# One more convolution pair through the seven-product form of a Trainium2 decoder trunk, with the recurrent heads, the token blocks and one held copy moved to fit

## The chip, the cores and the metric

The kernel runs on one core of a Trainium2 chip. The metric is the device time of one execution in microseconds (us). Two kinds of time appear below: the time of whole runs, and the span of one profiled execution, which is the trace that all rows come from. In the trace PE is TensorE's matmul row and PEld its weight loads, DVE is VectorE, ACT is ScalarE, POOL is GpSimd, and SP is SyncE, whose queue here does nothing but issue DMAs. A line such as L725 is a line of the kernel before.

## The reference

One decoder layer in float32 over 1024 tokens of width 1024:

```python
h = rms_norm(x, g_mix)
va, ga, xb, gb, sa, sb = split(h @ w_in + b_in)        # 1024, 1024, 1536, 1536, 1024, 1024 columns
u = silu(layer_norm(causal_conv31(va * sigmoid(ga))))   # width 31, depthwise
y_a = u @ w_a_out
v = rg_lru(causal_conv4(xb))                            # 16 heads of 96: two gates, then a linear scan
y_b = (v * gelu(gb)) @ w_b_out
x = x + (sigmoid(sa) * y_a + sigmoid(sb) * y_b) @ w_o
h = rms_norm(x, g_mlp)
x = x + square(relu(h @ w_1)) @ w_2
out = rms_norm(x, g_final)
```

The gates of `rg_lru` are two block-diagonal products with a sigmoid; the scan's decay is an exponential of one gate, and its input is scaled by a square root.

## The kernel before, in words

**Precision.** Every float32 operand is split into a high part and a low part (`float32r`), and a product is made of three matmuls: high by high, high by low, low by high. A matmul has a moving operand of 128x512. The high part is a copy on ACT. The low part is made in one of two ways: by a subtraction on DVE, or by `split_dma` (L63), which writes the negated source with ACT, adds the source to it with an accumulating DMA that POOL issues (L66), and then makes the high copy with a second ACT pass. The first way costs one ACT pass and one DVE pass, the second two ACT passes and a DMA.

**The in-projection, first part.** `w_in` has 56 column tiles of 128. The list `CH` (L686) orders those that are done one at a time; a turn `s` of the loop at L810 does one of them with 24 products for each half of the tokens, 48 matmuls (`chunk_mm`, L716). Three tiles are done before the loop, so the turns are 3 to 25. Column names are offsets (L427): VA and GA are the two sides of the gated convolution branch, XB the recurrent branch, GB, SA and SB the three gates. A turn also carries what follows from earlier tiles:

- an XB tile is copied out by two ACT passes in the next turn (`xb_out`, L468), convolved over 4 taps by DVE, and split by `xb_parts` (L489) in the turn after that;
- a GA tile gets its sigmoid on ACT in the next turn, and DVE multiplies it with the VA tile (`u_gate`, `u_mul`, `u_out`, L585 to L598), which makes one of eight convolution inputs `u`. The two last tiles stand in reverse order, GA ahead of VA (L689), so that the sigmoid is done while the last tile is multiplied;
- a recurrent head has two gate products. `HS0` (L796) names the turn in which each head's first product is issued, at the end of that turn; its second follows in the middle of the next turn, and both use one PSUM buffer, so each waits for ACT's sigmoid of the one before (`head_mm`, `head_gate`, L526 and L537);
- four heads make a group. In the turn after a group's last head (`EXP`, L799) ACT does the exponentials and tanh (`scan_exp`), a turn later the square roots (`scan_root`), and DVE does three `scan_tile`s (L573) in the turns after that;
- DVE's free time is filled with the taps of the width-31 convolutions (`conv`, L602), some 47 instructions each.

**Token blocks.** The second part multiplies 2x2 blocks of tokens by 2x2 blocks of weights with Strassen's seven products. It needs differences of token blocks: `x_load` (L662) fetches four blocks for each of two halves `c2` from a DRAM copy through SP's queue, `x_sum` (L668) does four DVE subtractions, and `x_parts` (L673) splits blocks 7, 6, 5 and 4. `XS` (L800) places these steps in the last five turns, and `ZX` (L1021) places the three last ones beside the first products of the second part.

**The in-projection, second part.** `ZPAIRS` (L729) lists pairs of column tiles, 15 of them, of which the seventh is the convolution pair VA+7 with GA+7. A pair takes 7 products of 12 matmuls (`z_mm`, L921). `zseq` (L779) writes out the order of the products, the first two pairs interleaved: products 1, 1, 2, 2, 6, 7, 7, 5, 6, 3, 4, 5. Weight sums are DVE work (`z_sums`), the splits of the left operands are `z_lhs` (L763), issued four products ahead, and `z_post` (L992) copies and evacuates.

**What sets the order.** Every engine executes its instructions in the order of the program text (a manual schedule). A small planner keeps a clock for PE, ACT and DVE, and uses it only to choose how many convolution taps go between the DVE steps that must be done (`later`, `vector_work`, L695 and L699). The pool `acts` (L36) has 37 buffers of 128x1024; when a tile is asked for, its first writer waits for the last user of the buffer it gets. The PSUM pool of the first part has three two-bank buffers under the tag `ps` and one under `ps2`, which the heads use (L47); its tags lie one after another in the order of their first use, and the second part's eight banks lie over them.

**The down-projection.** From L2143 the MLP's second product is done in seven products as well, for two halves `q2` of the tokens. The result of the first product, in `d0a`, is copied to `d0b` (`down_add`, L2016), and the second product then goes on adding into `d0a`. The copy of half 1 is kept in `held` and issued a step later. In steps m = 2, 3 and 4 of group 0 (`joint`) a held step that meets an even step is issued late, after the operand splits of that step and after the first half's matmuls.

Of the kernel before, what the change touches and what calls it, by code (L numbers as in the profile page):

```python
# [12 lines left out]
AF = mybir.ActivationFunctionType  # L13
ALU = mybir.AluOpType
# [5 lines left out]
NH = 16  # L20
# [10 lines left out]
def trunk_kernel(ctx: ExitStack, tc: tile.TileContext, x, xt_in, xt_eo, vecs, w_in, w_a_out, w_b_pl, w_b_sq,  # L31
                 w_rg, w_o, w_1, w_2, g_final, out):

    nc = tc.nc
# [9 lines left out]
    def T(name, dt=F32, shape=(P, S)):  # L44
        return tp.tile(list(shape), dt, tag="T", name=name)

    def PS(name, tag="ps"):  # L47
        return pp.tile([P, S], F32, tag=tag, name=name, bufs=1 if tag == "ps2" else 3)
# [286 lines left out]
    with tc.manual_schedule(engines={mybir.EngineType.Activation, mybir.EngineType.DVE,  # L335
                                     mybir.EngineType.PE}):
        warm = cp.tile([P, 10], F32, name="warm")
        nc.vector.memset(warm[:, 0:2], 1.0)
        nc.scalar.activation(warm[:, 0:1], warm[:, 1:2], AF.Sqrt)

        spare = PS("spare", "ps2")

        def idle_mm(n):
            for _ in range(n):
                nc.tensor.matmul(spare[:, 0:P], ones, ones, start=True, stop=True)

        idle_mm(13)
        rb["tile"] = PS("rb", "ps2")
        first_w(0, "h")
        first_w(0, "l")  # L350
        for c in range(8):
            x_plain(c)
            x_plain_low(c)
            if c == 7:
                first_w(1, "h")
                first_w(1, "l")
            for which in ("hh", "lh", "hl"):
                first_z(0, 0, c, which)
        for k in range(8):
            first_z(1, 0, k, "hh")  # L360
            first_z(1, 0, k, "hl")
        decay_on(6)
        first_w(2, "h")
        first_w(2, "l")
        decay_on(14)
        for t in range(4, 8):
            x_square(t, nc.scalar)
        for k in range(8):
            first_z(1, 0, k, "lh")
        x_root(1)  # L370
        decay_on(5)
        for k in range(8):
            first_z(2, 0, k, "hh")
            first_z(2, 0, k, "hl")
            if k == 4:
                x_spread(1)
        for k in range(8):
            first_z(2, 0, k, "lh")

        for c in range(9):  # L380
            if c < 8:
                x_scaled(1, c)
            else:
                x_root(0)
                x_spread(0)
            if 3 <= c < 7:
                x_square(c - 3, nc.scalar)
            if c:
                for which in ("hh", "lh"):
                    first_z(0, 1, c - 1, which)  # L390
                x_low(1, c - 1)
                first_z(0, 1, c - 1, "hl")
                for i in range(1, N0):
                    first_z(i, 1, c - 1, "hh")
                    first_z(i, 1, c - 1, "hl")
        for i in range(1, N0):
            for k in range(8):
                first_z(i, 1, k, "lh")
        decay()
        nc.vector.tensor_scalar(cab2, cab_c, 2.0, None, ALU.mult)  # L400
        pairs = caw[:, 8:].rearrange("p (i o j) -> p i o j", o=2, j=8)
        nc.vector.tensor_tensor(csum, pairs[:, :, 0, :], pairs[:, :, 1, :], ALU.add)
# [32 lines left out]
    def at(e, cost, ready=0.0):  # L435
        clk[e] = max(clk[e], ready) + cost
        return clk[e] + 0.1
# [144 lines left out]
    yd = dp.tile([8, P, S], F32, name="yd")  # L582
    ysum = []

    def u_gate(j, ps):  # L585
        ut[j] = u = T(f"u{j}")
        nc.scalar.activation(u.rearrange("p (o n) -> p o n", o=2), ps.rearrange("p (n o) -> p o n", o=2),
                             AF.Sigmoid, bias=bin_c[:, GA + j:GA + j + 1])
        return at("A", 1.11)

    def u_mul(j, ps, ready=0):
        uv = ut[j].rearrange("p (o n) -> p o n", o=2)
        later(ready, 1.28, nc.vector.scalar_tensor_tensor, uv, ps.rearrange("p (n o) -> p o n", o=2),
              bin_c[:, VA + j:VA + j + 1], uv, ALU.add, ALU.mult)
        fresh.append(j)

    def u_out(j, psv, psg):
        u_mul(j, psv, u_gate(j, psg))  # L598

    NE = WA // 2 + 1  # L600

# [71 lines left out]
    def x_parts(c2, *ps):  # L673
        for p in ps:
            src = xq[c2][{6: 22, 7: 12, 5: 11, 4: 21}[p]]
            xbh[p][c2] = h = T(f"xs{p}h_{c2}", F32R)
            xbl[p][c2] = l = T(f"xs{p}l_{c2}", F32R)
            if c2 == 0 and p < 6:
                split_dma(src, h, l)
                at("A", 2.0)  # L680
            else:
                nc.scalar.activation(h, src, AF.Copy)
                later(at("A", 1.0), 1.2, nc.vector.tensor_tensor, l, src, h.bitcast(F32),
                      ALU.subtract)

    CH = [XB, VA, GA, XB + 1, XB + 2, VA + 1, GA + 1, XB + 3, XB + 4, XB + 5, VA + 2, GA + 2]  # L686
    CH += [XB + t for t in range(6, 12)] + [c for j in range(3, 7) for c in (VA + j, GA + j)]
    NU = 7
    CH[-2:] = CH[:-3:-1]  # L689
    NC1 = len(CH)  # L690
    zps = {n: z0[n] for n in range(N0)}
    wraw, wst = {}, {}
# [2 lines left out]
    def later(ready, cost, f, *a):  # L695

        todo.append((ready, len(todo), cost, f, a))
# [28 lines left out]
                                 start=n == 0, stop=n == 23)  # L726
        at("P", len(halves) * (n1 - n0) * MM)

    ZPAIRS = [GB + 2 * i for i in range(6)] + [VA + 7] + [SA + 2 * i for i in range(4)]  # L729
    ZPAIRS += [SB + 2 * i for i in range(4)]  # L730
    NZ = len(ZPAIRS)
    zraw, zs, zo, zb = {}, {}, {}, {}
# [58 lines left out]
    def z_get(n, f):  # L791
# [1 line left out]

    ENGINES = {mybir.EngineType.Activation, mybir.EngineType.DVE, mybir.EngineType.PE,
               mybir.EngineType.SP, mybir.EngineType.Pool}
    HS0 = [4 + n + (n > 3) + (n > 7) for n in range(NH)]  # L796
    head_at = {s: n for n, s in enumerate(HS0)}

    EXP = {head_slot: g for g, head_slot in enumerate(HS0[4 * g + 3] + 1 for g in range(4))}  # L799
    XS = {NC1 - 5: ((x_load, 0),), NC1 - 4: ((x_sum, 0),), NC1 - 3: ((x_load, 1), (x_parts, 0, 6)),  # L800
          NC1 - 2: ((x_sum, 1), (x_parts, 0, 7, 5)), NC1 - 1: ((x_parts, 0, 4), (x_parts, 1, 6))}
    made = []
    head_w(0)
    w_load(3)
# [4 lines left out]
    with tc.manual_schedule(engines=ENGINES):  # L809
        for s in range(3, NC1):  # L810
# [31 lines left out]
            if c >= XB:  # L842
                xb_out(c - XB, zps[s - 1])
            elif c >= GA:
                if CH[s] == c - GA + VA:
                    u_gate(c - GA, zps[s - 1])
                else:
                    u_out(c - GA, zps[s - 2], zps[s - 1])
            w_parts(s + 1)
            if before is not None:  # L850
                head_gate(before, 1, clk["P"] - (2 * (24 - mid) + 6) * MM)
# [166 lines left out]
        elif p == 4:  # L1018
            z_out(i, 1, 0, zb[i, "u"], "c")

    ZX = {0: ((x_parts, 1, 7),), 2: ((x_parts, 1, 5),), 4: ((x_parts, 1, 4),)}  # L1021
    H_AT = {2: (0, 0), 5: (1, 1), 3: (0, 1), 4: (1, 0)}
    with tc.manual_schedule(engines=ENGINES):

# [152 lines left out]
        vector_work(clk["V"])  # L1177
        z_get(2, z_lhs)
        z_get(3, z_lhs)
        u_mul(NU - 1, zps[NC1 - 1])  # L1180
        vector_work(clk["V"])
        z_h(0, 0, 0)
        for n in range(len(zseq) + 2):
# [949 lines left out]
    with tc.manual_schedule(engines={mybir.EngineType.Activation, mybir.EngineType.DVE,  # L2133
                                     mybir.EngineType.PE}):
        for n, (g, p, kk) in enumerate(dseq[:-2]):
            m = n % 14
            end = g == NC_ - 1
            nx, nx2 = dseq[n + 1], dseq[n + 2]
            if m in DLOADS and not end:
                d_load(g + 1, *DLOADS[m])  # L2140
            elif m == 0:
                d_load(g, *DFIRST)
            if n == 0:  # L2143
                for q2 in range(2):
                    acc[0, 0, q2] = x_block(0, 0, q2)
            if (g, m) in XADD:
                xbs[g, m] = x_block(*XADD[g, m])
            joint = not g and m in (2, 3, 4)
            if held and not (joint and kk == 0):
                held.pop()()  # L2150
            lows_ = []
            if not end or m < 10:
                lows_.append(left_high(*nx))
            sums_ = d_sums(g, m)
            if sums_ and not joint:
                d_sum(*sums_.pop(0))
            if not end or m < 10:
                lows_.append(right(*nx2))
            down_mm(g, p, kk, 0)
            if joint:  # L2160
                for f in lows_:
                    f()
                if held:
                    held.pop()()
                for x in sums_[::-1]:
                    d_sum(*x)
            if kk:
                if end and p == 7:
                    d_last(0)
                else:  # L2170
                    down_add(g, p, 0)
            if not joint:
                for f in lows_:
                    f()
                for x in sums_:
                    d_sum(*x)
            if (g, m - 4) in XADD:
                k = XADD[g, m - 4]
                tt(acc[k], acc[k], xbs.pop((g, m - 4)), ALU.add)
            down_mm(g, p, kk, 1)  # L2180
# [101 lines left out]
```

## Time and profile before

| | |
|---|---|
| median of 3 runs | 1532.88 us (1532.06 to 1533.77) |
| the profiled execution | 1532.83 us, its span 1531.0 us |
| matmuls | 6722, PE busy 1519.7 us |
| first part's loop | from 43 to 339.1 us of the span |
| second part | 339.1 to 625.8 us |
| granted TensorE clock | 0.998 |

Times inside the trace are counted from the start of the span. Rows of the timeline give start, duration, engine, line, operation, tiles (with buffer numbers left out), and in brackets how long the engine was idle before and what ended that. Successive matmuls of 512 columns start 0.227 us apart, although each has a latency of 0.39 us.

### The profile page before, as it was taken

The page shows a single profiled execution, that of the slowest core. Times are in us where ns is not written, and L with a number is a line of the kernel's source. Part 1 is how long each engine was busy: PE and PEld are TensorE (multiplying, and loading weights), DVE is VectorE, ACT ScalarE, POOL GpSimd, SP SyncE. Part 2 cuts the span into 40 slices and gives each one's busy share as a digit, 9 for nine tenths or more (in the row PEclk, how much of TensorE's full clock was granted, in tenths as well). Part 3 has the DMA queues.
Part 4 walks back from the last instruction along what each step waited for, and adds up shares of the span by engine and source line. Part 5 has one row for each costly group of instructions (what it writes and reads, how often), then busy time and mean ns, then how long its engine had stood idle before and what let it go on. Part 6 is the DMA issues. An engine that isn't in the chain of part 4 may idle for free.

```text
span 1531.0 us, 18964 instructions
## 1 busy us (share of the span) xinstructions
PE 1519.7 (99%) x6722; PEld 1250.9 (82%) x6722; DVE 1200.4 (78%) x1636; ACT 928.2 (61%) x1299; POOL 192.3 (13%) x228
## 2 busy tenths in 40 slices
PE   9999999999999999999999999999999999999998
PEld 7878887888888888888888887888888878888886
DVE  6999996998999997788768879755555386777777
ACT  6748688576566667645475777554444445545475
POOL 0111011022222222000022332000000000101010
PEclk9999999999999999999999999999999999999999
DMA  9766778697997789863779897333333974776465
GB/s 351 189 145 158 180 171 190 200 257 211 265 257 175 183 207 280 295 224 124 265 194 301 191 209 193 129 129 112 112 113 111 305 254 126 182 206 169 108 123 153
DMA packets 130799, 296.53 MB, mean 194 GB/s; under 512 B 12896, under 2 KB 34912, under 8 KB 130704
## 3 DMA queue, kind: packets, MB, share of 16 engines
q1 hardware_dynamic: 98960, 215.92, 41.5%
q0 software_dynamic: 31600, 79.15, 28.1%
q8 instruction: 52, 0.85, 0.2%
q14 instruction: 43, 0.35, 0.1%
q10 hardware_dynamic: 144, 0.26, 0.0%
HBM read 149.79 MB, written 60.82 MB: 138 GB/s over the span
## 4 chain that ended last, share of the span: by engine, by line
PE 95%; issue 2%; DMA 1%; DVE 1%; ACT 1%; POOL 1%; SPq 0%; POOLq 0%; DVEq 0%; ACTq 0%
PE z L725 16%; PE z L258 2%; PE d2b L2002 2%; PE d1b L2002 2%; PE d0b L2002 2%; PE d3b L2002 2%; PE d0e L2002 1%; PE d3a L2002 1%; PE d2e L2002 1%; PE d2a L2002 1%; PE d1e L2002 1%; PE d1a L2002 1%; PE d3e L2002 1%; PE rg L532 1%; PE rg L534 1%
## 5 line engine op out<-in xcount | busy, mean ns | idle before, releaser
L725 PE MATMUL z<-xh,win_h 128*128 128x512 f32 x368 | 115.4, 391 | 0.0
L725 PE MATMUL z<-xl,win_h 128*128 128x512 f32 x368 | 114.9, 390 | 0.0
L637 DVE SCALAR_TENSOR_TENSOR y<-u,vec,y 128x511 f32<-128x511 f32 (+14 forms) x120 | 88.6, 738 | 0.0
L725 PE MATMUL z<-xh,win_l 128*128 128x512 f32 x368 | 87.4, 389 | 0.0
L637 DVE SCALAR_TENSOR_TENSOR yt<-u,vec,yt 128x511 f32<-128x511 f32 (+6 forms) x112 | 82.8, 739 | 0.0
L637 DVE SCALAR_TENSOR_TENSOR y<-yt,csum,y 128x511 f32<-128x511 f32 (+6 forms) x112 | 82.8, 739 | 0.0
L725 PEld LDWEIGHTS z<-xh,win_h 128*128 128x128 f32 x368 | 69.1, 188 | 16.0 <-ACT win_h L67 0.4
L725 PEld LDWEIGHTS z<-xl,win_h 128*128 128x128 f32 x368 | 69.1, 188 | 15.0
L725 PEld LDWEIGHTS z<-xh,win_l 128*128 128x128 f32 x368 | 69.1, 188 | 14.6
L542 ACT ACTIVATE g<-rg,vec 96x1024 f32<-96x1024 f32 x32 | 35.5, 1110 | 72.9 <-PE rg L534 72.8
L1697 ACT ACTIVATE o<-s 128x512 fp32r<-128x512 f32 x56 | 33.7, 623 | 45.7 <-DVE s L1681 26.4
L66 POOL DMA_DIRECT2D zo<-zw x45 | 39.2, 871 | 134.1 <-ACT zo L65 114.8
L483 DVE SCALAR_TENSOR_TENSOR v<-xb,vec,v 128x1023 f32<-128x1023 f32 (+2 forms) x36 | 46.2, 1283 | 6.3 <-ACT v L474 5.4
L66 POOL DMA_DIRECT2D db_10l<-br x4 | 3.5, 876 | 341.3 <-DMA br<-in_w_dram 254.4
L66 POOL DMA_DIRECT2D win_l<-win_raw x23 | 20.0, 867 | 194.0 <-ACT win_l L65 159.2
L65 ACT ACTIVATE zo<-zw 128x512 fp32r<-128x512 f32 x45 | 28.2, 627 | 24.3 <-PE z2f L929 2.1
L1219 DVE TENSOR_TENSOR o<-s,o 128x512 fp32r<-128x512 f32 x56 | 37.3, 684 | 1.3 <-ACT o L1697 1.3
L66 POOL DMA_DIRECT2D zo<-zs x30 | 26.4, 879 | 76.1 <-ACT zo L65 64.1
L67 ACT ACTIVATE zo<-zw 128x512 fp32r<-128x512 f32 x45 | 27.9, 621 | 0.0
L578 DVE TENSOR_TENSOR_SCAN g<-a,g 128x1024 f32<-128x1024 f32 x12 | 27.5, 2292 | 0.4
L66 POOL DMA_DIRECT2D ga<-gsa x8 | 7.0, 874 | 161.0 <-DMA m<-mbd 150.8
L1219 DVE TENSOR_TENSOR o<-w_raw,o 128x512 fp32r<-128x512 f32 x38 | 25.9, 684 | 0.0
(3182 smaller groups left out, 4913.1 us busy)
## 6 DMA issues: line engine op xcount, KB each, us to landing
w_raw<-in_w_dram SPq DMA_DIRECT2D x34, 512.0 KB, 5.5
br<-in_w_dram SPq DMA_DIRECT2D x32, 512.0 KB, 6.0
ar<-fd SPq DMA_DIRECT2D x32, 512.0 KB, 7.1
zw<-in_w_in_dram SPq DMA_DIRECT2D x28, 512.0 KB, 6.7
win_raw<-in_w_in_dram SPq DMA_DIRECT2D x23, 512.0 KB, 4.8
win_l<-win_raw POOLq DMA_DIRECT2D x23, 512.0 KB, 4.8
zo<-zw POOLq DMA_DIRECT2D x45, 256.0 KB, 5.4
gates<-zg SPq DMA_DIRECT2D x32, 256.0 KB, 4.0
```

Of the source, the lines that this page charges most:

```text
L65: nc.scalar.activation(l, src, AF.Copy, scale=-1.0)
L66: nc.gpsimd.dma_start(l, src, accum_op=ALU.add)
L67: nc.scalar.activation(h, src, AF.Copy)
L258: nc.tensor.matmul(z0[i][:, HALVES[hf]], w0[i][w][:, k, :], xpart(a, hf, k), start=k == 0 and which == "hh", stop=k == 7 and which == ("hl ...
L483: nc.vector.scalar_tensor_tensor(v[:, d:S], a[:, 0:S - d], cbw_c[:, w * 12 + t:w * 12 + t + 1], v[:, d:S], ALU.mult, ALU.add)
L542: nc.scalar.activation(a, gps.pop((n, gi))[:HD, :], AF.Sigmoid, bias=(ba_c, bx_c)[gi][:, n:n + 1])
L578: nc.vector.tensor_tensor_scan(i, a, i, 0.0, ALU.mult, ALU.add)
L637: nc.vector.scalar_tensor_tensor(o[:, k:], a[:, 0:HS - k], c, o[:, k:], ALU.mult, add)
L725: nc.tensor.matmul(zps[s][:, HALVES[hf]], w[:, k, :], xw[k][part][hf], start=n == 0, stop=n == 23)
L1219: tt(l, src, h.bitcast(F32), ALU.subtract)
L1697: nc.scalar.activation(o[:, 0], src, AF.Copy)
L2002: nc.tensor.matmul(o, a, b, start=start and n == 0, stop=stop and n == len(todo) - 1, skip_group_check=not start or not stop)
```

## The change

- the convolution pair VA+6 with GA+6 leaves `CH` and becomes a second convolution pair in `ZPAIRS`, seventh there, with VA+7 now ninth. The first part has 24 tiles in place of 26, the second 16 pairs in place of 15;
- XB+6, XB+7 and XB+8 move ahead of VA+2 and GA+2; the gap in `HS0` after head 7 goes, so heads 8 to 15 come one turn earlier, at turns 13 to 20;
- the two last tiles stand in their usual order, and `u_gate` and `u_mul` are one function again; its last call, after the loop, now does the sigmoid too;
- the token blocks are loaded, summed and split one turn later against the end of the first part, all blocks of `c2` = 0 are split by `split_dma`, and six `x_parts` steps in place of three go beside the second part's first six products;
- the twelfth `scan_tile` no longer fits into a turn, and goes to the second part's step 6;
- the spare PSUM tile of the warm-up is taken from `ps`;
- the held copy is issued at once in step m = 2 of the down-projection (in step 4 it stays late).

```diff
-        spare = PS("spare", "ps2")
+        spare = PS("spare")
...
-            if c2 == 0 and p < 6:
+            if c2 == 0:
                 split_dma(src, h, l)
...
-    CH = [XB, VA, GA, XB + 1, XB + 2, VA + 1, GA + 1, XB + 3, XB + 4, XB + 5, VA + 2, GA + 2]
-    CH += [XB + t for t in range(6, 12)] + [c for j in range(3, 7) for c in (VA + j, GA + j)]
-    NU = 7
-    CH[-2:] = CH[:-3:-1]
+    CH = [XB, VA, GA, XB + 1, XB + 2, VA + 1, GA + 1, XB + 3, XB + 4, XB + 5, XB + 6, XB + 7, XB + 8]
+    CH += [VA + 2, GA + 2, XB + 9, XB + 10, XB + 11] + [c for j in range(3, 6) for c in (VA + j, GA + j)]
+    NU = 6
...
-    ZPAIRS = [GB + 2 * i for i in range(6)] + [VA + 7] + [SA + 2 * i for i in range(4)]
+    ZPAIRS = [GB + 2 * i for i in range(6)] + [VA + 6, SA, VA + 7] + [SA + 2 * i for i in range(1, 4)]
...
-    HS0 = [4 + n + (n > 3) + (n > 7) for n in range(NH)]
+    HS0 = [4 + n + (n > 3) for n in range(NH)]
...
-    XS = {NC1 - 5: ((x_load, 0),), NC1 - 4: ((x_sum, 0),), NC1 - 3: ((x_load, 1), (x_parts, 0, 6)),
-          NC1 - 2: ((x_sum, 1), (x_parts, 0, 7, 5)), NC1 - 1: ((x_parts, 0, 4), (x_parts, 1, 6))}
+    XS = {NC1 - 4: ((x_load, 0),), NC1 - 3: ((x_sum, 0),), NC1 - 2: ((x_load, 1), (x_parts, 0, 6)),
+          NC1 - 1: ((x_sum, 1), (x_parts, 0, 7))}
...
-                if CH[s] == c - GA + VA:
-                    u_gate(c - GA, zps[s - 1])
-                else:
-                    u_out(c - GA, zps[s - 2], zps[s - 1])
+                u_out(c - GA, zps[s - 2], zps[s - 1])
...
-    ZX = {0: ((x_parts, 1, 7),), 2: ((x_parts, 1, 5),), 4: ((x_parts, 1, 4),)}
+    ZX = {0: [(x_parts, 1, 6)], 1: [(x_parts, 1, 7)], 2: [(x_parts, 0, 5)], 3: [(x_parts, 1, 5)], 4: [(x_parts, 0, 4)], 5: [(x_parts, 1, 4)]}
+    ZX.setdefault(6, []).append((later, 0, 4.8, scan_tile, 11))
...
-        u_mul(NU - 1, zps[NC1 - 1])
+        u_out(NU - 1, zps[NC1 - 2], zps[NC1 - 1])
...
-            if held and not (joint and kk == 0):
+            if held and not (joint and m == 4):
                 held.pop()()
```

More of the change, by code (lines that the diff above doesn't have):

```diff
@@ L583, in trunk_kernel, with u_out @@
     ysum = []
[L585 to L594, printed above, removed]
+    def u_out(j, psv, psg):
+        u = T(f"u{j}")
+        uv = u.rearrange("p (o n) -> p o n", o=2)
+        nc.scalar.activation(uv, psg.rearrange("p (n o) -> p o n", o=2), AF.Sigmoid,
+                             bias=bin_c[:, GA + j:GA + j + 1])
+        later(at("A", 1.11), 1.28, nc.vector.scalar_tensor_tensor, uv,
+              psv.rearrange("p (n o) -> p o n", o=2), bin_c[:, VA + j:VA + j + 1], uv,
+              ALU.add, ALU.mult)
+        ut[j] = u
         fresh.append(j)
-    def u_out(j, psv, psg):
-        u_mul(j, psv, u_gate(j, psg))
     NE = WA // 2 + 1
```

## The prediction

> **What bounds the kernel now.** I read the page first, then PE's waits, then the chain that ended last.
>
> ```profile
> span 1531.0 us, 18964 instructions
> PE 1519.7 (99%) x6722; PEld 1250.9 (82%) x6722; DVE 1200.4 (78%) x1636; ACT 928.2 (61%) x1299; POOL 192.3 (13%) x228
> ...
> PE spare L345 <- POOL ones L113: 1.6, 1, 1.6
> PE d0a L2002 <- ACT d0b L2016: 1.4, 1, 1.4
> PE f0d L1709 <- DMA o<-s: 0.6, 1, 0.6
> ...
> 301.14 38.13 PE z L725 x168
> ...
> 448.97 2.72 PE z6a L929 x12
> ```
>
> PE is busy for 99% of the span and its waits are few and short; the three longest stand here. The chain rows say what a matmul costs: 168 of the first part take 38.13 us, 0.227 each; the 12 of one Strassen product take 2.72. So time is gained here by fewer matmuls or by one of those waits, and lost wherever another engine's cover runs out. The profiled execution took 1532.83 us, 0.05 under the median of 1532.88, and I make the sum against it.
>
> **The change: the matmuls.** Two column tiles of 48 matmuls go and a pair of 7 x 12 comes: 96 - 84 = 12 fewer, **-2.72**. The second part has no PE wait in the trace, and the new pair is of a kind that stands there already. It costs DVE about 6 us more (ten half-width passes near 0.7, less one full multiply of 1.26):
>
> ```profile
> 240.00:280.00 40.00, 40.00 (x177) 31.91 (x176) 24.85 (x32) 35.42 (x37) 5.24 (x6) 1.00 0.80 183
> 580.00:625.80 45.80, 45.80 (x203) 37.93 (x203) 30.36 (x38) 35.07 (x55) 9.60 (x11) 1.00 1.07 312
> ```
>
> These are windows: DVE (the third busy figure, after PE and PEld; the first figure is the window's length) is idle for 15.2 us in the first, where no convolution input is ready, and for 15.4 us at the end of the second part. The later of these hides 6 us, and convolutions 6 and 7 with it. I cost it at nothing; without that cover it costs what overflows (a rival below).
>
> **The held copy.**
>
> ```profile
> 1227.57 0.61 PE L2002 MATMUL d0a<-db_11l,da_11h 128*128 128x512 f32 x2
> 1230.29 0.61 PE L2002 MATMUL d0a<-db_20l,da_20h 128*128 128x512 f32 x2
> 1232.35 0.50 PE L2002 MATMUL d0a<-db_20h,da_20h 128*128 128x512 f32 x1 [1.44 <-ACT d0b L2016]
> 1235.20 0.39 PE L2002 MATMUL d0a<-db_21h,da_21h 128*128 128x512 f32 x1
> ...
> 1230.32 1.06 ACT L1930 ACTIVATE db_60h<-t 128x1024 fp32r<-128x1024 f32 x1 [1.81 <-DVE t L1900]
> 1231.29 1.01 ACT L2016 ACTIVATE d0b<-d0a 128x1024 f32<-128x1024 f32 x1
> 1231.34 1.22 DVE L1219 TENSOR_TENSOR da_21l<-ar,da_21h 128x1024 fp32r<-128x1024 f32 x1
> ```
>
> The copy of half 1 stands on ACT behind a split that waits 1.81 us for DVE, though its source is complete at about 1228.2. PE would have gone on at 1230.75 and starts at 1232.35, and the next 12 matmuls take 2.85 in place of 2.72: 1.60 + 0.13 = **-1.73**. Issued at once, the copy ends near 1229.2, 1.5 us ahead of its use. It pushes one ACT split (da_21h) by 1.8 us to 1230.2; the low part that reads it starts on DVE at 1231.34 anyway and ends at 1232.56, and PE, now earlier, wants it at 1233.47. Covered by 0.9.
>
> **Heads closer.** Group 2's exponentials used to meet no XB tile in the turn after; now the turn with the square roots also copies out XB+11. In the old trace the turn that begins at 253 is that turn without the copy.
>
> ```profile
> 242.30 1.10 ACT L471 ACTIVATE xb<-z,vec 128x1024 f32<-128x1024 f32 x1
> 244.58 1.05 ACT L65 ACTIVATE win_l<-win_raw 128x1024 fp32r<-128x1024 f32 x1
> 258.26 1.05 ACT L65 ACTIVATE vtl<-v 128x1024 fp32r<-128x1024 f32 x1
> 262.05 1.09 ACT L542 ACTIVATE g<-rg,vec 96x1024 f32<-96x1024 f32 x1
> 265.27 0.40 PE L532 MATMUL rg<-vth,rgh 96*96 96x512 f32 x1
> 268.98 1.11 ACT L542 ACTIVATE g<-rg,vec 96x1024 f32<-96x1024 f32 x1
> 272.12 0.40 PE L532 MATMUL rg<-vth,rgh 96*96 96x512 f32 x1
> DMA to landing us min/median/max: 4.6/5.3/7.7
> ```
>
> The copy-out takes ACT 244.58 - 242.30 = 2.28. The gate that frees the heads' PSUM buffer then ends at 263.14 + 2.28 = 265.42, where PE wants it at 265.27; the next one at 272.37, against 272.12. **+0.3** for both. The last row is the landing of the split's DMA (vtl, 12 of them): head 13 now reads a split of its own turn, begun at 258.26; about 1.3 to the issue plus 5.3 is 264.9, ahead of 265.7; at the longest, 7.7, it is 1.6 late. I take the median, and keep 1.6.
>
> **The start of the second part.** The last turns repeat the old ones one tile (10.88 us) earlier, so I keep the old clock and let the second part begin at 339.10 - 10.88 = 328.22.
>
> ```profile
> 314.71 1.23 DVE L575 SCALAR_TENSOR_TENSOR g<-a,g 128x1024 f32<-128x1024 f32 x1 [0.58 <-ACT g L566]
> 319.73 1.28 ACT L587 ACT_TABLE_LOAD   x1 [2.21 <-DVE g L578]
> 320.68 4.99 DVE L462 TENSOR_TENSOR xs<-xs,xs 128x1024 f32<-128x1024 f32 x4
> 321.02 1.12 ACT L587 ACTIVATE u<-z,vec 128x1024 f32<-128x1024 f32 x1
> 322.04 1.05 ACT L65 ACTIVATE win_l<-win_raw 128x1024 fp32r<-128x1024 f32 x1
> 325.59 1.22 DVE L575 SCALAR_TENSOR_TENSOR g<-a,g 128x1024 f32<-128x1024 f32 x1
> 330.44 1.26 DVE L462 SCALAR_TENSOR_TENSOR u<-z,vec,u 128x1024 f32<-128x1024 f32 x1
> 339.10 0.39 PE L929 MATMUL z0a<-xh,zo 128*128 128x512 f32 x1
> 339.43 0.69 DVE L462 TENSOR_TENSOR zs<-zs,zw 128x512 f32<-128x512 f32 x1
> 354.56 0.63 ACT L65 ACTIVATE zo<-zs 128x512 fp32r<-128x512 f32 x1
> 355.63 0.88 POOL L66 DMA_DIRECT2D zo<-zs  x1 [2.60 <-ACT zo L65]
> 364.94 0.62 PE L929 MATMUL z0e<-xh,zo 128*128 128x512 f32 x2
> 340.15:354.56 14.41, 14.41 (x66) 11.91 (x65) 13.66 (x19) 11.43 (x18) 1.76 (x2) 1.00 0.80 217
> DMA to landing us min/median/max: 3.6/6.4/7.1
> ```
>
> The sigmoid of u4, with its table load, now stands ahead of the square roots: 322.04 - 319.73 = 2.31. So scan tile 9 starts at 314.71 + 2.3 = 317.0 and, taking 4.85 (325.59 to 330.44), ends at 321.9; x_sum to 326.8, scan tile 10 to 331.6; two weight sums of 0.7 to 333.0, which is 4.8 after the start. Before, the second sum ended at 340.12, 1.0 after the start. ACT waits for it with product 6's split, and from there to product 3's split (354.56) it had 11.43 us of work in the window. It now has four more full passes (five added, one gone) of 0.95: 15.2. Product 3's split begins at 4.8 + 15.2 = 20.0, POOL issues its DMA 1.07 later (354.56 to 355.63), and it lands a median 6.4 on (last row, POOL's DMAs of this stretch): 27.5. PE wants it at 364.94 - 339.10 = 25.84. That is 1.6 late, and **+1.6** is my term; at 3.6 it is nothing and at 7.1 it is 2.3. Product 6's low part, by the same sum 4.8 + 1.0 + 6.4 = 12.2 against 11.8, lies inside it. After step 6 ACT's extra passes end and the 2.4 us that it had in hand come back.
>
> [...]
>
> **Costed at nothing.** Scan tile 11 in step 6 (4.85 on DVE) displaces convolution taps. VA+2 coming three turns later leaves DVE without taps for some 12 us near 190 (my estimate, about one turn of 10.88), and the hole at 255 closes for it. SP passes the four z loads ahead of the second x_load (a rival). The spare tile decides which PSUM banks the last tiles hold: by order of use the second part's first banks are free, and the one under the last GA tile is wanted at product 3 of the sequence, 5.4 us on, when its sigmoid (2.4) is over. If the first bank were that one, 2.4 at most.
>
> **Sum:** 1532.83 - 2.72 - 1.73 + 0.3 + 1.6 = **1530.3**.
>
> **Rivals.** *All of it hidden:* DMAs land near 3.6, the heads' gates just fit; 1532.83 - 4.45 = 1528.4. For it: PE waits nowhere in this stretch before. Against: ACT's 2.4 us in hand are less than the 4.0 it loses.
>
> *The x blocks come late:* they used to be issued ahead of the four z loads and now stand behind them.
>
> ```profile
> L666 SPq DMA_DIRECT2D xs<-xu x4: 319/376/897, 305.5 to 308.3; - x4
> DMA to landing us min/median/max: 11.9/12.7/13.8
> ```
>
> The first row is the four blocks' issue, the second the landing of those z loads. Issued 2.8 later (311.1) with 13.8, the last block lands at 324.9, 3.0 after x_sum wants it, and scan, sums, split and DMA all move: 1.6 + 3.0, giving 1533.3. Against: one weight load fewer is in flight. It would show as DVE waiting for xs.
>
> *Slower: DVE overflows.* If DVE's 12 us hole near 190 is not repaid at 255, 12 + 6 = 18 go to the second part, 2.6 beyond its 15.4 idle; and if the layer norm, which needs all eight convolutions, then has no slack, PE waits at L1427. It decides from 15.4 us of pushed work; with both holes lost (12 + 6 + the last x steps near 6) it is 8.6 late: 1530.3 + 8.6 = 1538.9. Against: the 15.2 us hole at 240 to 280.
>
> **How the numbers follow.** The forecast has 0.36, between 1529.0 and 1531.8 by its terms' bounds; all hidden 0.34, since the landings spread evenly about the one that decides; late blocks 0.14 (1531.8 to 1535); slower 0.16, since it has three covers to lose. A measurement can tell about 0.2% (3.07 us) from no change, so faster is below 1529.8: all of the second case and a third of the first, 0.46. Slower, above 1535.9, is the last, 0.16; the rest is 0.38. The range, 1527.8 to 1535.0, leaves out the slower case and a little on both sides: 2 in 10.
>
> **What would show it.** Matmuls at L725 fewer by 96, at L929 more by 84; no wait of PE on ACT d0b; gaps of 0.1 to 0.3 ahead of rg in the turns at 256 and 270; PE waiting once for a zo DMA in the second part's first 30 us, 1.6 or less. A wait at xs or at L1427, or a PE gap elsewhere before 625, proves me wrong, and so does d0b's copy still ending a wait.

## The result and the profile after

The changed kernel takes **1544.74 us** (median of five runs, 1541.76 to 1546.64) against 1532.88 before (a median of five runs as well, 1532.06 to 1533.77): 11.9 us slower, a ratio of 1.0076 with a 95% interval of 1.0064 to 1.0087. The forecast was 1530.3, and the range ended at 1535.0. The profiled execution took 1546.64 us, 1.9 above the median, its span is 1544.9 against 1531.0, so the two traces differ by 13.9.

From the page after:

```profile
span 1544.9 us, 18999 instructions
PE 1522.0 (99%) x6710; PEld 1249.7 (81%) x6710; DVE 1202.3 (78%) x1643; ACT 936.8 (61%) x1316; POOL 196.4 (13%) x233
```

The longest waits of PE (engine, tile and line; what it waited for; us in total, times, longest):

```profile
PE z0a L925 <- DMA zo<-zw: 2.9, 1, 2.9
PE z0a L925 <- ACT z0b L991: 2.1, 1, 2.1
PE z3e L925 <- DMA zo<-zs: 2.1, 1, 2.1
PE z6e L925 <- DMA zo<-zs: 1.9, 1, 1.9
PE z15e L925 <- DMA zo<-zs: 1.6, 1, 1.6
...
PE z14f L925 <- DMA zo<-zw: 1.5, 1, 1.5
```

Names such as z0a and z3e are accumulators of the second part in PSUM, and the number is that of the pair, counted from 0; `zo` is a left operand, made from weights (`zw`) or from a weight sum (`zs`). The 12 matmuls are gone (6722 - 6710), and no row on d0b is left. In its place stand six waits of the second part, which had none: 12.1 us in all, five of them on a DMA that makes the low part of a left operand. The next view gives their times (start, duration, engine, line, operation, tiles; in brackets the idle time before):

```profile
317.64 0.39 PE L925 MATMUL z0a<-xh,zo 128*128 128x512 f32 x1
...
321.20 0.73 PE L925 MATMUL z0a<-xh,zo 128*128 128x512 f32 x2 [2.95 <-DMA zo<-zw]
...
329.06 0.50 PE L925 MATMUL z0a<-xh,zo 128*128 128x512 f32 x1 [2.13 <-ACT z0b L991]
...
413.00 0.73 PE L925 MATMUL z3e<-xh,zo 128*128 128x512 f32 x2 [2.10 <-DMA zo<-zs]
...
472.29 0.73 PE L925 MATMUL z6e<-xh,zo 128*128 128x512 f32 x2 [1.88 <-DMA zo<-zs]
...
622.60 0.73 PE L925 MATMUL z14f<-xs4h,zo 128*128 128x512 f32 x2 [1.52 <-DMA zo<-zw]
...
635.85 0.73 PE L925 MATMUL z15e<-xh,zo 128*128 128x512 f32 x2 [1.63 <-DMA zo<-zs]
```

The second part begins at 317.64. Two column tiles of 10.88 earlier than 339.10 would be 317.34, so the heads cost 0.3, as forecast. Then come two waits at the border of the two parts, two in the middle, two at the end.

Behind two of the six, PE runs slower for a while. In the windows of the next view the first number is the length, then PE's busy time with its instructions; the number after the five engines is PE's granted clock.

```profile
326.44:329.85 3.41, 1.28 (x6) 0.74 (x5) 3.04 (x4) 3.41 (x6) 0.87 (x1) 1.00 1.10 302
329.86:333.27 3.41, 3.41 (x9) 2.63 (x8) 3.41 (x5) 3.41 (x5) 0.49 (x1) 0.50 0.71 168
469.81:473.21 3.40, 1.52 (x7) 0.96 (x6) 2.59 (x5) 2.09 (x4) 0.87 (x1) 1.00 0.86 202
473.22:476.63 3.41, 3.41 (x10) 2.64 (x9) 2.44 (x4) 0.42 (x1) 0.00 (x0) 0.50 0.88 216
633.65:637.04 3.39, 1.76 (x7) 1.15 (x8) 2.43 (x4) 3.39 (x5) 0.00 (x0) 1.00 1.09 282
637.06:640.46 3.40, 3.40 (x16) 2.80 (x16) 2.54 (x3) 2.45 (x4) 0.00 (x0) 1.00 1.03 404
```

In the second and the fourth row PE is busy throughout at a clock of 0.50, and does 9 or 10 matmuls where the last row has 16: half of 3.41, 1.7 us, lost each time, and no list of waits shows it.

The account between the traces, from the starts of the first matmuls of each stage: at the first product of the next stage (yb0b) the changed kernel is 15.37 us late. With -2.72 for the matmuls and +0.30 for the heads, the second part lost 17.8. The waits in brackets are 12.4 of it and the clock is 3.4; the rest, about 0.3 at each wait, is that the profile counts a wait from the modelled end of the matmul before it (0.39 after its start, where the next is due at 0.227) and that the first pair after a wait takes 0.73. By place, with the clock: 7.2 at the border, 2.4 and 3.8 in the middle, 4.2 at the end; 0.1 more is spread thinly. Afterwards the held copy brings back 1.74, and the rest is within 0.3.

**Why a low part was late in the middle.** POOL issues these DMAs. In the changed kernel, ahead of the wait at 413.00, the timeline of POOL has:

```profile
398.82 1.19 POOL L650 DMA_DIRECT2D ysum<-y  x1
401.57 0.87 POOL L66 DMA_DIRECT2D zo<-zs  x1 [1.55 <-ACT zo L65]
```

and the view of this one tile gives the time from the issue of the last row's DMA to its landing:

```profile
DMA to landing us min/median/max: 11.4/11.4/11.4
```

A convolution has ended: at 398.82 POOL adds its 512 KB to a running sum (`ysum`) with an accumulating DMA, and SP has sent the tile itself to DRAM (`yd`) 1.5 us earlier. The split of product 3 is issued 2.8 later and lands after 11.4, at 412.95; PE starts at 413.00. POOL was idle for 1.55 us ahead of this issue, so it is not POOL's own time that makes the split late. The median of this kind is 5.9 between 340 and 560 us. The kernel before, at the same kind of end, and below it the landing of its split:

```profile
377.59 0.87 POOL L66 DMA_DIRECT2D zo<-zs  x1 [1.85 <-ACT zo L65]
378.13 1.23 POOL L650 DMA_DIRECT2D ysum<-y  x1
```

```profile
DMA to landing us min/median/max: 7.7/7.7/7.7
```

Here the split stands ahead of the sum. The changed kernel has the bad order at 398.8 and at 459.7 (split at 460.69, landed after 11.6), and these are its two waits in the middle. So the first theory is **A: transfers that run just ahead of a split's DMA make it late.** The rivals: **B: ACT and DVE are short of time in the second part**, since it has one pair more; and for the border **C: the order of ACT's work** (the sigmoid and its table load ahead of the square roots) sets the waits.

### The profile page after: what moved, and what is told of

The parts are those of the page before. It is cut to its first block, busy times and chain, and to the rows that moved or that the text cites. A ratio compares the mean times of both kernels' runs of the same rounds, so it can differ in the third digit from the quotient of the medians.

```text
span 1544.9 us, 18999 instructions
## 1 busy us (share of the span) xinstructions
PE 1522.0 (99%) x6710; PEld 1249.7 (81%) x6710; DVE 1202.3 (78%) x1643; ACT 936.8 (61%) x1316; POOL 196.4 (13%) x233
## 4 chain that ended last, share of the span: by engine, by line
PE 85%; DMA 6%; issue 3%; DVE 3%; ACT 2%; POOL 1%; SPq 0%; POOLq 0%; DVEq 0%; ACTq 0%
PE z L724 10%; PE d2b L1999 2%; PE d1b L1999 2%; PE d0b L1999 2%; DMA zo<-zs 2%; PE d3b L1999 2%; DMA xs<-xu 1%; PE d0e L1999 1%; PE d3e L1999 1%; PE d3a L1999 1%; PE d2e L1999 1%; PE d2a L1999 1%; PE d1e L1999 1%; PE d1a L1999 1%; PE d0a L1999 1%
## 5 line engine op out<-in xcount | busy, mean ns | idle before, releaser
L724 PE MATMUL z<-xh,win_h 128*128 128x512 f32 x336 | 105.5, 391 | 0.0
L724 PE MATMUL z<-xl,win_h 128*128 128x512 f32 x336 | 105.0, 390 | 0.0
L724 PE MATMUL z<-xh,win_l 128*128 128x512 f32 x336 | 79.9, 389 | 0.0
L724 PEld LDWEIGHTS z<-xh,win_h 128*128 128x128 f32 x336 | 63.1, 188 | 14.7 <-ACT win_h L67 0.4
L724 PEld LDWEIGHTS z<-xl,win_h 128*128 128x128 f32 x336 | 63.1, 188 | 13.7
L724 PEld LDWEIGHTS z<-xh,win_l 128*128 128x128 f32 x336 | 63.1, 188 | 13.4
L65 ACT ACTIVATE zo<-zw 128x512 fp32r<-128x512 f32 x48 | 30.0, 625 | 24.5 <-PE z7f L925 2.1
L67 ACT ACTIVATE zo<-zw 128x512 fp32r<-128x512 f32 x48 | 29.8, 621 | 0.0
L65 ACT ACTIVATE zo<-zs 128x512 fp32r<-128x512 f32 x32 | 20.0, 626 | 13.6 <-DVE zs L462 8.2
```

What stands on the lines that cost most here:

```text
L65: nc.scalar.activation(l, src, AF.Copy, scale=-1.0)
L724: nc.tensor.matmul(zps[s][:, HALVES[hf]], w[:, k, :], xw[k][part][hf], start=n == 0, stop=n == 23)
```

## The experiments

"Before" is the kernel before, run beside each kernel on the same chip; a ratio is to it, with its 95% interval.

**1. The held copy alone.**

```diff
-            if held and not (joint and kk == 0):
+            if held and not (joint and m == 4):
```

> The kernel before with the held copy's edit alone. If the copy of half 1 stood in the wrong place and nothing is late behind it, the PE wait of 1.60 us on d0b and the 0.13 us after it go: 1532.9 - 1.7 = 1531.1 us. If another split takes the place of the copy (da_21h is pushed back by 1.8 us), PE waits there and the time stays within 0.5 us of 1532.9.

Measured: 1531.21 us against 1532.99, a ratio of 0.9988 (0.9979 to 0.9996), 1.78 less. The copy and what follows it on ACT:

```profile
1227.71 1.01 ACT L2016 ACTIVATE d0b<-d0a 128x1024 f32<-128x1024 f32 x1 [0.94 <-PE d0a L2002]
1228.63 1.05 ACT L1919 ACTIVATE da_21h<-ar 128x1024 fp32r<-128x1024 f32 x1
```

The copy ends at 1228.7, PE needs it at 1230.2, 1.5 us later as the prediction had it, and PE no longer waits there. This edit is right by itself, and this kernel is the fastest of all that ran.

**2. No running sums.** The changed kernel without the accumulating DMAs of the convolutions after the first, so the layer norm's mean lacks seven parts.

```diff
-        else:
-            nc.gpsimd.dma_start(ysum[0], acc, accum_op=add)
```

> The changed kernel without the accumulating DMAs that add a finished convolution to the running sum (all but the first), so the layer norm's mean is wrong and 7 DMAs of 512 KB are missing. Theory A, that these transfers delay the DMAs which make the low parts of the second part's left operands: the waits at product 3 of pairs 3 and 6 go (2.3 us, and 2.0 us with 1.7 us of half clock behind it), the last two (1.7 and 2.1 us) shrink, and the start of the second part loses something, since one sum is issued 23 us ahead of it: 1531 to 1537 us. Theory B, that ACT and DVE are late in the second part by their own work: within 1 us of 1544.7.

Measured: 1533.07, a ratio of 1.0002 (0.9993 to 1.0011): 11.7 less than the changed kernel. PE's waits:

```profile
PE f1d L1704 <- DMA o<-s: 1.5, 1, 1.5
PE z0a L923 <- DMA zo<-zw: 0.9, 1, 0.9
PE z0a L923 <- ACT z0b L989: 0.9, 1, 0.9
PE z0f L923 <- DVE zc L462: 0.4, 1, 0.4
```

The waits in the middle and at the end are gone, those at the border shrink from 5.1 to 1.8 (one sum was issued at 294.5, 23 us ahead of it), and the clock never drops. All the compute is as it was, so B falls.

**3. The sums behind the split.** The changed kernel, whole; a convolution's end is kept in a list and issued right behind the next product 3's split.

```diff
             z_get(n + 4, z_lhs)
+            if n + 4 < L and zseq[n + 4][1] == 3:
+                flush_ends()
```

> The changed kernel, whole, in which a convolution that ends in the second part issues its store and its sum right behind the DMA of the next product 3, not when it ends. Theory A: the two waits in the middle go (6.0 us with the half clock), the last ones may, the start of the second part stays: 1535 to 1539 us. Theory B: 1544.7 within 1 us, or slower, since each finished tile holds its buffer for up to 19 us longer.

Measured: 1540.42, ratio 1.0050 (1.0036 to 1.0064), 4.3 less than the changed kernel, but 1.4 above the range that A was given. Its POOL rows at the same place, and the landing of the split:

```profile
401.97 0.87 POOL L66 DMA_DIRECT2D zo<-zs  x1 [2.60 <-ACT zo L65]
402.51 1.23 POOL L657 DMA_DIRECT2D ysum<-y  x1
```

```profile
DMA to landing us min/median/max: 8.7/8.7/8.7
```

The sum now follows 0.54 us behind, so the same bytes are moved at the same place. With the order turned round the split lands after 8.7, and both waits in the middle go (one of 0.4 comes on z4a), as A said. The border stays (3.0 and 0.8), and at the end the waits change their place (1.2 on z15e, 1.0 on yb0b).

**4. The same, the wrong way round, in the kernel before.** Here `flush_ends()` stands ahead of `z_get(n + 4, z_lhs)`.

> The kernel before, whole, in which a convolution that ends in the second part issues its store and its sum right ahead of the DMA of the next product 3. Theory A: the waits come to this kernel too, 1 to 2 us at each of the four or five ends and 1.7 us more where the clock halves: 1537 to 1546 us. Theory B: 1532.9 within 0.5 us.

Measured: 1542.62, ratio 1.0062 (1.0046 to 1.0077), 9.6 slower. POOL's rows ahead of a product 3, the landing of the split, and PE's longest waits:

```profile
393.90 1.23 POOL L657 DMA_DIRECT2D ysum<-y  x1
396.69 0.87 POOL L66 DMA_DIRECT2D zo<-zs  x1 [1.56 <-ACT zo L65]
```

```profile
DMA to landing us min/median/max: 12.3/12.3/12.3
```

```profile
PE z2e L940 <- DMA zo<-zs: 2.6, 1, 2.6
PE z14e L940 <- ACT zc L1017: 2.4, 1, 2.4
```

The first of these waits is A's, and so is one of 0.6 on z5e: same products, same work, another place for two DMAs. For the middle of the second part A is shown from both sides.

The second wait, on zc, is not a late split. ACT's pass for zc stands behind the pass wbp0h, and this row has the wait that decides; below it stands the landing of the finished convolution's store (`yd`), which is issued at 613.41:

```profile
624.85 1.06 ACT L1045 ACTIVATE wbp0h<-wbp 128x1024 fp32r<-128x1024 f32 x1 [5.34 <-issue]
```

```profile
DMA to landing us min/median/max: 11.4/11.4/11.4
```

The store lands at 624.8, and ACT goes on at 624.85. The row names no releaser ("issue"), but in the trace the semaphore that ACT waits for until then is this store's. So a convolution that is sent off late also holds its buffer longer, and here the next writer of that buffer waits 5.34 us for it. Each of the two long waits brought a stretch at half clock as well. With it, by the starts of the matmuls, the first place lost 4.9 us, z5e 0.9, and the one on the buffer 4.3: well over a third of the 9.6 is not A's.

**5 to 8. The border.** All four stand on run 3 (1540.42).

> The third run (ends issued behind product 3), in which also the convolution that ends 23 us ahead of the second part keeps its store and its sum back until the second part's first product 3 is issued. Theory A, late transfers at the border: most of the 6.1 us that this place still costs there goes: 1535 to 1538 us. Theory C, ACT's order at the border (the sigmoid and its table load ahead of the square roots) sets these waits: 1540.4 within 1 us.

Edit: `held_ends[0] = s > NC1 - 4` in the first part's loop, so the sum that was issued at 294 us is now issued at 339.6. Measured: 1542.95, ratio 1.0062 (1.0047 to 1.0077): a miss. The first splits now land after a median of 7.1 and the first wait is gone, but two others stand behind it in PE's waits:

```profile
PE z0f L937 <- DVE zc L462: 2.5, 1, 2.5
PE z0a L937 <- ACT z0b L1003: 2.1, 1, 2.1
```

> The third run, in which the second four token blocks are loaded one turn earlier, so ahead of the four weight loads in SP's queue. Theory A: they land before DVE wants them, and the second wait of the border (0.8 us) with the half clock after it goes; the first (3.0 us, on a split's DMA) stays or shrinks: 1537 to 1540 us. Theory C: 1540.4 within 1 us. If the buffers of the pool acts aren't free that early, the loads wait in SP's queue and push the weight loads back: slower than 1540.4.

Edit: `(x_load, 1)` from turn NC1 - 2 to NC1 - 3. Measured: 1548.43, ratio 1.0100 (1.0085 to 1.0115). It is the third branch, though the place is another: ACT, not SP, waits for a buffer. PE's longest wait, and ACT's row ahead of it:

```profile
PE z L735 <- ACT win_h L67: 9.3, 1, 9.3
```

```profile
312.09 1.28 ACT L595 ACT_TABLE_LOAD   x1 [12.02 <-DMA hd<-g]
```

The sigmoid of u asks for a buffer whose last user is the store of a scan (hd), and this store stands behind the loads in SP's queue; the next weight split waits behind the sigmoid, and PE for it. The four early blocks have taken the buffers that were free. The wait brings 10.24 us at half clock.

> The third run, in which DVE makes the low parts of the first half's blocks 6 and 7 again, as in the kernel before, so two accumulating DMAs of 512 KB fewer are issued by POOL between the first splits of the second part, and ACT has two passes fewer. Theory A: the first wait (3.0 us on the DMA of product 1's split, which is issued just behind the first of them) shrinks by 2 or more: 1536 to 1539 us. Theory C: two ACT passes, so 1.9 us less in the chain: also faster, but by the wait for ACT, not by the first. If DVE's 2.4 us more count: slower than 1540.4.

Edit: `if c2 == 0 and p < 6:` as before. Measured: 1538.67, ratio 1.0038 (1.0025 to 1.0051), as A expected: the first wait goes. Five of 0.6 to 1.3 are left, on ACT, DVE and two late DMAs.

> The third run with all three of these edits. Theory A: no wait over 0.5 us at the border; what is left over 1528.7 (the time before less 2.7, less 1.8, plus 0.3) are the waits at the second part's end, 1 to 3 us: 1529.5 to 1533 us. Theory C: above 1535.

Measured: 1555.70, ratio 1.0144 (1.0127 to 1.0160), a miss: run 6's wait is in it (8.1), and with the end at 294 us kept back, as in run 5, so is the one on DVE's sum zc (4.7 here, 2.5 there).

**9. The order of the tiles alone, in the kernel before.** XB+6 to XB+8 ahead of VA+2 and GA+2, and nothing else.

> The kernel before with one edit: XB+6, XB+7 and XB+8 stand ahead of VA+2 and GA+2, and nothing else moves. It asks what put the ends of the convolutions onto the splits. If the hole that this leaves on DVE near 190 us (about 15 us, three tiles without a new convolution input) isn't repaid before the second part, the later ends move by that against the products, and some fall just ahead of a product 3's DMA: 1535 to 1541 us. If DVE's idle 15 us between 240 and 280 us takes it up: 1532.9 within 0.7 us, and the shift comes from the shorter first part alone.

Measured: 1533.43 against 1532.99, ratio 1.0001 (0.9991 to 1.0010). The ends in the second part stand where they stood, to 0.3 us. DVE's windows (the third busy figure):

```profile
180.00:220.00 40.00, 40.00 (x177) 32.24 (x176) 24.91 (x26) 32.73 (x35) 5.26 (x6) 1.00 0.76 189
...
240.00:280.00 40.00, 40.00 (x176) 31.93 (x176) 37.41 (x50) 35.61 (x37) 5.24 (x6) 1.00 0.76 176
```

The hole near 190 us is there, and the one from 240 to 280 (24.85 busy before) closes for it. So the reorder is free, and the ends of the changed kernel are moved by the rest: the part that is 21.8 us shorter and the pair that joins the second. Which share each has was not tried.

**10. The sums on DVE.** The changed kernel, whole; one DVE pass in place of the accumulating DMA.

```diff
-            nc.gpsimd.dma_start(ysum[0], acc, accum_op=add)
+            nc.vector.tensor_tensor(ysum[0], ysum[0], acc, add)
```

> The changed kernel, whole, in which DVE adds a finished convolution to the running sum (one pass of 1.2 us, 7 of them) in place of POOL's accumulating DMA of 512 KB. Theory A: the same as leaving the sums out, 1533.1, within 1.5 us. Theory B (DVE is what is short): slower than the changed kernel, 1545 us or more, since DVE has 8.6 us more to do.

Measured: 1532.93, ratio 1.0001 (0.9992 to 1.0011), the same as leaving the sums out. DVE has the seven passes (1.23 us each) to spare. The run also parts the sum from the store: the split of pair 3's product 3 is issued at 397.80, 4.6 us behind the same store (4.2 in the changed kernel), and this is its landing:

```profile
DMA to landing us min/median/max: 9.0/9.0/9.0
```

So with no sum it lands after 9.0, with the sum just behind it after 8.7 (run 3), with the sum ahead of it after 11.4, and PE has room for about 9 (the 11.4 less the wait of 2.10). In the middle it is the sum that counts, and its place in POOL's order. PE's waits in run 10:

```profile
PE f1d L1707 <- DMA o<-s: 1.2, 1, 1.2
PE z0a L926 <- DMA zo<-zw: 1.0, 1, 1.0
PE z0a L926 <- ACT z0b L992: 0.8, 1, 0.8
```

This repairs most of the loss: 11.8 of the 16.0 us between 1544.7 and what the arithmetic promised (1533.0 - 2.7 - 1.8 + 0.3 = 1528.7). What is left is mostly the border, which loses 3.3 there. So the repaired kernel is no faster than the one before, and 1.7 slower than the held copy alone (run 1).

**11 to 15. What is left at the border.** All on run 10 (1532.93).

> The run before this one, in which DVE also makes the low parts of the first half's blocks 6 and 7, as in the kernel before. Theory A: the first splits of the second part land earlier, its first two waits (0.9 us each) go, and one on DVE or ACT of about 1 us stays: 1530.5 to 1532.5 us. Theory C, that ACT's order at the border is the bound: 1533 or more.

Measured: 1534.19, ratio 1.0007 (0.9997 to 1.0016): a miss for A, and within what C was given. The two first waits went, and four others of 0.7 to 1.3 came within 30 us (z0e on ACT's copy, z0e and z1e on splits, z0f on zc).

> The same, with block 5 of the first half split by DVE too, and the last scan tile at step 12 of the second part in place of step 6, where it stood ahead of the sum of product 5 that PE waited for (1.2 us). Theory A: only waits under 0.5 us are left in the second part, so the 4.2 us (two column tiles less a pair, the held copy, the heads) come out: 1529 to 1531 us. If DVE's 2.4 us more delay the weight sums: 1532 or more, with a wait at product 5 or 6.

Measured: 1540.21, ratio 1.0037 (1.0024 to 1.0050): the slower branch, though the longest wait stands elsewhere. A split at the border is late by 2.9, and at the end z15b waits 1.8 for ACT, where conv 7 ends at 624.5 in place of 600.7.

> The run with the sums on DVE (1532.9 us), in which block 6 of the first half is split behind the first two left operands and not ahead of them, so that POOL issues their DMAs about 1.5 us sooner and none of 512 KB runs ahead of them. If the order decides: the first wait (1.2 us) goes and nothing comes in its place: 1531.5 to 1532.2 us. If the amount decides: the wait comes back at product 6, which needs block 6, or at z0b: 1532.5 or more.

Edit: `(x_parts, 0, 6)` into the step behind the first two left operands. Measured: 1533.89, ratio 1.0005 (0.9995 to 1.0014). The first wait goes, the second grows from 0.8 to 2.1, as the second branch had it.

> The run before this one, in which the last scan tile goes to step 12, and the splits of block 4 one step later. If the order decides: the wait on DVE's sum zc (0.5 us) goes as well: 1531.0 to 1531.8 us. If the amount decides: a wait on block 4 or a later one appears, 1532.5 or more.

Measured: 1533.97, ratio 1.0005 (0.9996 to 1.0015): the wait on z0b stays at 2.1, and one of 0.8 on a split takes the place of zc's. The time is that of the second branch, but block 4 is not what PE waits for.

> The run before this one, in which scan tile 10 too goes into the second part, to step 3, so that the two weight sums for product 6 no longer wait behind it on DVE, nor ACT behind them with the copy z0b. If the order decides: no wait over 0.3 us at the border is left and the whole 4.2 us come out, less what the layer norm's stage varies by: 1529 to 1531 us. If the amount decides: DVE is late with blocks 6 and 7 instead, 1532.5 or more.

Measured: 1535.04, ratio 1.0009 (0.9999 to 1.0018): z0b's wait goes, and the DMA of a split takes its place with 1.8, where the second branch had DVE late. In this trace 1.8 more are lost far behind the border (gu1a, on the DMA of another split), with a stretch at half clock, so not all of the time is the border's.

Three arrangements of the same work (13 to 15) and two with more of it on DVE (11, 12) all give waits of some 2 to 5 us at the border or the second part's end, each time on another engine. Runs 10, 11, 13 and 14 lie within 1.3 us of each other with intervals that overlap, so which of them is best isn't shown; what is read here are the waits of one trace each. They fit the amount, not one order: what the first part no longer carries is pushed over the border, where ACT and DVE are both busy (in the changed kernel for 3.41 and 3.04 of the 3.41 us from 326.44) and splits land late (the first four there after 10.0 to 13.5). This is argued, and that no order exists that fits isn't shown.

## Why the prediction was wrong, point by point

- **The matmuls** (-2.72): right. 12 fewer, and the products are the cheap ones.
- **The held copy** (-1.73): right, 1.78 by itself (run 1), and the cover named for the split behind it held.
- **Heads closer** (+0.3): right, also in its place: the gaps ahead of rg stand at 254.5 (0.3 with the pair behind it) and 261.5 (0.1), one tile earlier than the old trace's 265.3 and 272.1; the second part begins 0.30 after 317.34.
- **The new pair's DVE work, "I cost it at nothing"**: this is the step that failed, and the largest part of the loss (10.4 of 17.8). The idle 15 us at the end of the second part do hide the passes, and the layer norm never waited at L1427. But a convolution is not only passes. Its end issues a store and an accumulating DMA of 512 KB, and the step moves that end against the products: from 376.6 and 436.3 in the trace before to 397.3 and 458.2, where it stands just ahead of a split. That gave 2.4 and 3.8 in the middle and, with the last end at 610.8 in place of 586.9, most of the 4.2 at the end (run 2 has none of these). The prediction looked at whether the last end comes in time, and not at where each end falls.
- **The start of the second part** (+1.6): this term failed too, with 7.2 measured. The wait of ACT for the weight sum was there, but later (the sum was done 8.8 us after the start, where the prediction had 4.8), and the wait that the term prices, PE on product 3's split, never came: PE had stopped at two earlier places. Three things were off.

  The DMAs land later than the trace before had it. The first four splits of the changed kernel:

```profile
DMA to landing us min/median/max: 10.0/11.9/13.5
```

  Before, the same four had a median of 5.2, and the prediction took 6.4. So the wait came at the first product of the order, where the sum looked at the tenth: it followed the split of product 3, and PE already stood in product 1, behind its first two matmuls. What made these four late is more than one thing. The change gives blocks 6 and 7 of the first half to `split_dma`, and block 6's accumulating DMA of 512 KB is issued at 309.65, 1.5 us ahead of the first of the four; with DVE back on these blocks the first wait goes (run 7). It also goes with the end at 294 us kept back (run 5), and shrinks to 0.9 without the sums (run 2).

  The token blocks came later than in the rival. The wait of their loads in SP's queue, and their landing:

```profile
SPq L666 <- DMA hd<-g: 7.2, 1, 7.2
```

```profile
DMA to landing us min/median/max: 12.3/14.6/16.5
```

  The fourth load stands 7.2 us in SP's queue, because its buffer is still being stored by a scan; it lands at 319.2, which is 1.6 after the start, where the rival "the x blocks come late" had 3.3 ahead of it. So the blocks did come late, mostly through a buffer that the rival did not name. From 312 us on DVE waits 3.2 us for them in three waits, near the rival's 3.0; what this alone cost PE was not separated.

  And the wait was passed on by the order of ACT's work. ACT's rows at the border:

```profile
326.43 0.63 ACT L65 ACTIVATE zo<-zs 128x512 fp32r<-128x512 f32 x1 [7.48 <-DVE zs L462]
...
328.44 0.57 ACT L991 ACTIVATE z0b<-z0a 128x512 f32<-128x512 f32 x1
```

  ACT stands 7.48 us for the weight sum that DVE does behind the late blocks, and the copy z0b, which needs nothing of that, stands behind it. PE waits for this copy (2.13). The prediction named ACT's wait for the sum and what it does to product 3's split, but not the copy queued between them.

  On C: ACT's chain is not what set the border first (run 2 takes 4.8 of the 7.2 away without touching ACT), but it is what stands next (runs 5 and 13).
- **The clock** was in no term: two stretches of 3.41 us at half speed cost 3.4 us in all.
- **The rivals.** "DVE overflows" gave the right sign by the wrong mechanism: it needed the layer norm to wait. Its hole near 190 us is there (DVE is busy for 23.3 of the 40 us from 180 to 220), and run 9 shows that alone it is repaid and costs nothing.

## What to carry to other kernels

When a step moves, list the DMAs that it issues at its end and ask which accumulating or splitting DMA now follows them in the queues; a landing time taken from the old trace did not hold here for the new neighbours (6.4 was taken, and a median of 11.9 came). Where a stage boundary moves earlier without its surroundings getting lighter, expect the waits to move from engine to engine when one of them is repaired, as they did in runs 11 to 15, and take the parts of a change that stand by themselves (here the held copy, 1531.21 us) without the rest. Here a large transfer whose result is wanted much later, the sum of 512 KB, did better behind the small ones that PE waits for (run 3, sum and store, 4.3 us less than the changed kernel), or with its adding on an engine that had time to spare (run 10, 11.8 less).

## What the hardware showed that was not expected

**Half clock after a short wait.** PE's clock fell to 0.50 for 3.41 us at a time (for 10.24, three times that, in runs 6 and 8, and once for 6.83 in run 8), mostly without PE being idle for long. The two stretches of the changed kernel start 143.36 us apart, at 329.86 and 473.22, which is 42 steps of 3.413. Counted from such a stretch in these steps, the trace falls into windows; the six rows of windows above are cut at these places. After a window in which PE is busy for 1.28 or 1.52 the next has half clock, after one with 1.76 it hasn't. Run 15 lies between:

```profile
323.09:326.48 3.39, 1.59 (x7) 0.93 (x7) 3.39 (x5) 3.39 (x6) 0.00 (x0) 1.00 1.07 291
326.50:329.89 3.39, 3.39 (x10) 2.61 (x9) 1.23 (x3) 2.62 (x3) 0.87 (x1) 0.50 0.98 216
```

Nine of the traces had such a stretch. Cut into full windows of 3.413 us, they have 20 that were followed by half clock: 15 at full clock, in which PE was busy for 1.62 us or less, and 5 that were at half clock already, with 1.76 or less. In every other window of these traces, between the first and the last matmul, PE was busy for 1.79 or more. (In its full width the window shown with 1.59 has 1.62, and the one with 1.76 has 1.79.) The longer wait of 2.95 at 321.20 lies across two windows (PE is busy for 2.05 and 1.83 of them) and cost nothing beyond itself, while the 2.13 at 329.06 lies in one and cost 1.7 more. So in these traces a window at full clock in which PE is idle for 1.79 us, little more than half of it, was followed by half clock, and one with 1.63 idle (the one at 633.65) was not. A wait of 2 us cost 2 (2.10 at 413.00) or 3.8 (2.13 at 329.06), by where it fell. That might be one way for equal executions to differ; the five times of the changed kernel lie 4.9 us apart, those before 1.7. That the clock explains this spread wasn't tried.

**Landing times differed with the neighbours by a factor of two and more.** The same DMA of 256 KB landed after 3.3 us at its quickest, a median of 5.9, and 11.4 or 11.6 behind one sum of 512 KB and one store; at the border, behind four weight loads, a sum, two stores, four blocks and the DMA of block 6, after 10.0 to 13.5. The prediction took the old trace's median of 6.4, which was not near what the changed order gave.
